# Attention's probabilities scaled by their reciprocal sums before the transposing instead of after the product with V

## Chip, cores and metric

One core of one Trainium2 chip. The metric is the device time of one execution in microseconds (us), as the median of three runs of the same program.

## What is computed

Two layers of a backbone over 1024 latent tokens with a prefix of 256 context tokens, all in float32. Each layer: modulated RMSNorm, one input projection split into retention, latent attention and pooling, an output projection, then a gated MLP with a convolution of width 3. Only the attention matters here. Eight heads; 1024 latent queries see 1280 keys (256 context, 1024 latent), 256 context queries see the 256 context keys. In layer 1 only the latent queries are needed.

```python
def mla_attend(qn, qr, kn, kr, v):
    s = jnp.einsum('bhqd,bhkd->bhqk', qn, kn) + jnp.einsum('bhqr,bkr->bhqk', qr, kr)
    p = jax.nn.softmax(s.astype(jnp.float32) * MLA_SCALE, axis=-1)
    return jnp.einsum('bhqk,bhkd->bhqd', p.astype(v.dtype), v)
```

## The kernel before

Every float32 product is made of reduced-precision parts: an operand is split into a high part (a copy rounded to fp32r) and a low part (the difference), and TensorE multiplies the parts.

**The unit.** `attention` (L1640) works in units of one head and 256 queries, which are two tiles t = 0, 1 of 128 queries. Layer 0 has 40 units (five per head: four latent, one context), layer 1 has 32 (four per head). For a latent unit:

- `S0`, `S1`, `SC` (`score`, L1689, which calls `mm3`, L187): the scores with queries on partitions, into PSUM: `SL[t]` for the 1024 latent keys of one tile, `SC` for the 256 context keys of both tiles. There is one buffer of each.
- `M0`, `M1`, `MC` (L1708, L1711): row maxima on VectorE. `B0`, `B1` (L1716): the bias of the exponential from them.
- `X0`, `X1` (`expo`, L1722): ScalarE's exponentials into `P`, 128 x 1280 in SBUF, with the row sums as a by-product.
- `T00`, `T01`, `T10`, `T11`, `T12` (`trans`, L1738): TensorE turns P round in blocks of 128 x 128 into a PSUM tile `pt`; the first digit is the query tile, the second the group of four key blocks; `T12` takes the context keys of both tiles. `H..` (L1761): ScalarE's high part of `pt`. `L..` (L1766): VectorE's low part.
- `AVa`, `AVb`, `AVc` (`av`, L1789): 20 products with V into the PSUM tile `O` (V's high and low part side by side give 128 output rows).
- `RC`, `DG`, `RR`: the sums are put together and inverted on VectorE (L1772, L1774); GpSimd splits the inverses and puts them on a diagonal (L1782 to L1784); two matmuls with ones (L1806) spread them over 64 partitions, beside `O`.
- `LO` (L1812): ScalarE copies the lower half of `O`. `OU` (`out`, L1814): VectorE adds the halves (L1817) and multiplies by the spread inverses (L1822) into `op`.
- `PAh`, `PAl` (L1833, L1841): for an odd head, the high and low part of `op` for the output projection. `PAl` runs on VectorE and reads two tiles in SBUF.

`pt` and `O` share three PSUM banks in turn; every third allocation falls on the same bank.

**The order** is written out by hand in `ORDERS`: a string of `name:k`, where k is the unit's distance from the first unit of the step. A step covers two units in layer 1 and five in layer 0. Each engine takes its part of that string strictly in the order written. So around one unit TensorE does `AVc` of the unit before, three groups of transposing with `SC` of the next unit between or ahead of them, `S1` of the next unit, two groups of transposing, `AVa`, `S0`, `AVb`. GpSimd does nothing else in this stage, and no DMA is issued by it there; SyncE's queue loads the next head's Q, K and V.

Of the kernel before, what the change touches and what calls it, by code (L numbers as in the profile page):

```python
# [8 lines left out]
F32 = mybir.dt.float32  # L9
F32R = mybir.dt.float32r  # L10
AF = mybir.ActivationFunctionType
ALU = mybir.AluOpType
# [5 lines left out]
SEQ = 1024  # L18
CTX = 256
T = SEQ + CTX  # L20
# [37 lines left out]

ORDERS = (
# [15 lines left out]
)  # L75


# [84 lines left out]
class Net:  # L162
# [325 lines left out]
    def run(self):  # L488
        tc = self.tc
        with ExitStack() as es:  # L490
            es.enter_context(tc.manual_schedule())
            P = lambda name, bufs=1, **k: es.enter_context(tc.tile_pool(name=name, bufs=bufs, reuse_waits="tile", **k))
            self.cpool = P("const")
            self.big = P("big")
            self.wpool = P("w", 2)
            self.dram = es.enter_context(tc.tile_pool(name="dram", bufs=1, space=DRAM))
# [1143 lines left out]
    def attention(self, l):  # L1640
        tc, nc, a = self.tc, self.nc, self.a
        lat = l == L - 1
        Tq = self.Tq
        Y = self.Y
        with ExitStack() as es:
            ga = es.enter_context(tc.tile_pool(name="ga", bufs=1, reuse_waits="tile"))
# [4 lines left out]
            SC = pS.tile([128, 2, 256], F32, name="SC")  # L1651

            units = []
# [23 lines left out]
            st = Units()  # L1677

            def begin(u):
                s = type("U", (), {})()  # L1680
                s.P = [None, None]
                s.sm = ga.tile([128, 12], F32, tag="sm", name="sm", bufs=3)
# [6 lines left out]
            def score(u, t, out, kc, n):  # L1689
                h, q0, _ = units[u]  # L1690
                q, k, _ = heads[h]
                qs = slice(q0 + t * 128, q0 + t * 128 + 128)
                self.mm3(out, q[0][:, qs], q[1][:, qs], k[0][:, kc:kc + n], k[1][:, kc:kc + n], True, True)
# [28 lines left out]
            def expo(u, t):  # L1722
                s = st[u]
                sm = s.sm
                P = s.P[t] = ga.tile([128, T], F32, tag="P", name="P", bufs=3)
                b = sm[:, 4 + t:5 + t]
                if units[u][2]:
                    nc.scalar.activation(P[:, 0:SEQ], SL[t], AF.Exp, scale=ATT_SCALE, bias=b,
                                         accum_out=sm[:, 6 + t:7 + t])
                nc.scalar.activation(P[:, SEQ:T], SC[:, t], AF.Exp, scale=ATT_SCALE, bias=b,  # L1730
                                     accum_out=sm[:, 8 + t:9 + t])
# [33 lines left out]
                    hi, lo, ps = st[u].t[t, g]  # L1765
                    nc.vector.tensor_tensor(out=lo, in0=ps, in1=hi.bitcast(F32), op=ALU.subtract)  # L1766

            def recip(u):
                sm = st[u].sm
                src = sm[:, 8:10]  # L1770
                if units[u][2]:
                    nc.vector.tensor_tensor(out=sm[:, 6:8], in0=sm[:, 6:8], in1=src, op=ALU.add)  # L1772
                    src = sm[:, 6:8]
                nc.vector.reciprocal(out=sm[:, 10:12], in_=src)  # L1774

            def diag(u):

                s = st[u]
                rr = ga.tile([128, 2, 2], F32R, tag="rr", name="rr", bufs=2)
                s.dg = ga.tile([128, 2, 2, 128], F32R, tag="dg", name="dg", bufs=2)  # L1780
                r = s.sm[:, 10:12]
                nc.gpsimd.tensor_copy(rr[:, 0], r)  # L1782
                nc.gpsimd.tensor_tensor(out=rr[:, 1], in0=r, in1=rr[:, 0].bitcast(F32), op=ALU.subtract)
                nc.gpsimd.tensor_tensor(out=s.dg.rearrange("p i t q -> p (i t) q"),  # L1784
                                        in0=self.ident[:, None, :].to_broadcast([128, 4, 128]),
                                        in1=rr.bitcast(F32).rearrange("p i t -> p (i t)")[:, :, None].to_broadcast([128, 4, 128]),
                                        op=ALU.mult)

            def av(u, g):  # L1789
                s = st[u]  # L1790
# [8 lines left out]
                    nc.tensor.matmul(s.O[:, 0:256], v[:, k], s.pl[:, k], start=False, stop=k == 9)  # L1799
                    s.open = k < 9  # L1800

            def rep(u):

                s = st[u]
                for i in range(2):
                    nc.tensor.matmul(s.O[0:64, 256:512], self.onesr, s.dg[:, i].rearrange("p t q -> p (t q)"),  # L1806
                                     start=not s.open and i == 0, stop=not s.open and i == 1)

            def low_out(u):
                s = st[u]  # L1810
                s.t1 = ga.tile([64, 256], F32, tag="t1", name="t1", bufs=2)
                nc.scalar.activation(s.t1, s.O[64:128, 0:256], AF.Copy)  # L1812

            def out(u):  # L1814
                s = st[u]
                h, q0, _ = units[u]
                nc.vector.tensor_tensor(out=s.t1, in0=s.O[0:64, 0:256], in1=s.t1, op=ALU.add)  # L1817
                if h % 2 == 0 and q0 == 0:
                    st["op"] = ga.tile([128, Tq], F32, tag="op", name="op")
                op = ops["op", u] = st["op"]  # L1820
                r = slice(64 * (h % 2), 64 * (h % 2) + 64)
                nc.vector.tensor_tensor(out=op[r, q0:q0 + 256], in0=s.t1, in1=s.O[0:64, 256:512], op=ALU.mult)  # L1822
                del st[u]

            def part_high(u):
# [9 lines left out]
            def part_low(u):  # L1835
                h, q0, _ = units[u]
                op = ops.pop(("op", u))
                if h % 2 == 1:
# [9 lines left out]
                   "M0": lambda u: max_lat(u, 0), "M1": lambda u: max_lat(u, 1), "MC": max_ctx,  # L1848
                   "B0": lambda u: bias(u, 0), "B1": lambda u: bias(u, 1),
                   "X0": lambda u: expo(u, 0), "X1": lambda u: expo(u, 1),  # L1850
                   "RC": recip, "DG": diag, "RR": rep, "LO": low_out, "OU": out,
                   "PAh": part_high, "PAl": part_low}
            for g in range(3):
                ops["AV" + "abc"[g]] = lambda u, g=g: av(u, g)
# [425 lines left out]
```

## Time and profile before

| what | value |
|---|---|
| median of three runs | 3344.43 us (3340.59 to 3345.43) |
| the profiled execution: time, span | 3334.97 us, 3333.2 us |
| TensorE, mean granted clock | 0.968 |
| busy: PE, PEld, DVE, ACT, POOL | 95%, 80%, 64%, 39%, 12% |
| chain that ended last: PE, DVE, ACT, POOL | 78%, 10%, 5%, 2% |
| attention of layer 0 | 498.5 to 794.4 us |
| attention of layer 1 | 2219.2 to 2489.5 us |

PE is TensorE (matmul), PEld its weight loads, DVE VectorE, ACT ScalarE, POOL GpSimd, SP SyncE. In the lists, `out<-in` names the tiles by the program's names and L1806 is a line of the kernel. The bounds of the two attention stages are where the first and last of their instructions stand in the list by time.

### The profile page before, as it was taken

To read this page: it belongs to the slowest core of one execution; us is meant where nothing else is said; L and a number is where in the kernel's file an instruction comes from. 1 tells how busy PE (TensorE), PEld (TensorE's weight loads), DVE (VectorE), ACT (ScalarE), POOL (GpSimd) and SP (SyncE) were. 2 spreads that over 40 slices of the span, in tenths; PEclk is the share of its full clock that TensorE was granted. 3 is DMA by queue.
4 is the path that set the end of the run, shared out by engine and by line. 5 is a ranking of instruction groups with operands and counts; after the bars stand their busy time and mean duration, and the time that the engine had idled before them with its cause. 6 is when DMAs were issued, how large, how long until landed. Compare 5 with 4: busy or idle time off the path is not lost.

```text
span 3333.2 us, 43486 instructions
## 1 busy us (share of the span) xinstructions
PE 3171.5 (95%) x16873; PEld 2676.0 (80%) x16873; DVE 2143.8 (64%) x3720; ACT 1291.3 (39%) x2277; POOL 413.1 (12%) x557
## 2 busy tenths in 40 slices
PE   7989789999999999999999899789999999999998
PEld 4767668998878888888888787579988788888887
DVE  6434768987667666666665745669985655555556
ACT  7443447774332222222222423457762422222222
POOL 3550221121310000000000300221112100000000
PEclk8999869999999999999999999879999999999999
DMA  6531643222212222222221322542223111111111
GB/s 227 178 120 52 243 114 82 64 67 99 76 46 62 64 64 64 64 64 64 64 64 39 105 88 85 205 117 77 68 85 89 58 48 48 48 48 48 48 48 73
DMA packets 307464, 280.27 MB, mean 84 GB/s; under 512 B 28880, under 2 KB 274874, under 8 KB 307258
## 3 DMA queue, kind: packets, MB, share of 16 engines
q1 hardware_dynamic: 292778, 228.65, 23.3%
q0 software_dynamic: 9152, 35.91, 2.7%
q10 hardware_dynamic: 5328, 12.93, 1.0%
q8 instruction: 133, 2.18, 0.3%
q14 instruction: 73, 0.60, 0.1%
HBM read 219.51 MB, written 57.93 MB: 83 GB/s over the span
## 4 chain that ended last, share of the span: by engine, by line
PE 78%; DVE 10%; ACT 5%; issue 3%; POOL 2%; DMA 2%; SPq 0%; DVEq 0%; POOLq 0%; ACTq 0%
PE up L203 30%; PE ip L826 8%; PE dn L189 5%; PE dn L190 5%; PE dn L191 5%; PE pt L1745 4%; PE O L1798 2%; PE O L1799 2%; PE SL L189 2%; PE SL L190 2%; PE SL L191 2%; PE wo L189 2%; PE wo L191 2%; PE wo L190 2%; DMA mraw<-in_w_mod_dram 1%
## 5 line engine op out<-in xcount | busy, mean ns | idle before, releaser
L2086 DVE SCALAR_TENSOR_TENSOR x<-dn,mod,x 128x512 f32<-128x512 f32 (+1 forms) x448 | 306.1, 687 | 401.8 <-PE dn L191 401.4
L189 PE MATMUL dn<-ah,dh 128*128 128x512 f32 (+1 forms) x800 | 295.2, 369 | 2.6 <-DVE x L2086 2.6
L190 PE MATMUL dn<-al,dh 128*128 128x512 f32 (+1 forms) x800 | 294.7, 368 | 0.0
L191 PE MATMUL dn<-ah,dl 128*128 128x512 f32 (+1 forms) x800 | 294.4, 368 | 0.0
L203 PE MATMUL up<-yml,whi 128*128 128x512 f32 (+1 forms) x840 | 254.6, 368 | 0.0
L203 PE MATMUL up<-ym,wlo 128*128 128x512 f32 (+1 forms) x840 | 254.4, 368 | 0.0
L203 PE MATMUL up<-ym,whi 128*128 128x512 f32 (+1 forms) x840 | 254.4, 368 | 0.0
L2037 ACT ACTIVATE t<-up,vecs 128x1280 f32<-128x1280 f32 (+2 forms) x92 | 116.0, 1265 | 307.6 <-PE up L203 297.6
L2046 DVE SCALAR_TENSOR_TENSOR t<-up,vecs,t 128x1023 f32<-128x1023 f32 (+2 forms) x135 | 134.4, 995 | 144.4 <-ACT t L2037 144.3
L203 PE MATMUL up<-yp,whi 128*128 128x512 f32 (+1 forms) x840 | 220.6, 369 | 0.0
L203 PE MATMUL up<-yr,whi 128*128 128x512 f32 (+1 forms) x840 | 215.0, 370 | 5.1 <-ACT whi L178 5.1
L1766 DVE TENSOR_TENSOR ptl<-pt,pth 128x512 fp32r<-128x512 f32 x328 | 214.3, 681 | 1.3 <-ACT pth L1761 0.2
L251 POOL TENSOR_TENSOR wlo<-raw,whi 128x512 fp32r<-128x512 f32 (+1 forms) x10 | 16.4, 1659 | 1579.7 <-ACT whi L250 1579.7
L1761 ACT ACTIVATE pth<-pt 128x512 fp32r<-128x512 f32 x328 | 184.7, 600 | 44.1 <-PE pt L1745 40.7
L179 DVE TENSOR_TENSOR wlo<-raw,whi 128x1024 fp32r<-128x1024 f32 (+1 forms) x134 | 163.6, 1221 | 56.4 <-ACT whi L178 56.4
L1745 PE MATMUL pt<-cpack,P 128*128 128x128 f32 x1312 | 180.9, 275 | 3.6 <-DVE op L1822 2.5
L402 DVE SCALAR_TENSOR_TENSOR macc<-mraw,sc,macc 128x128 f32<-128x128 f32 x560 | 175.1, 357 | 7.0
L203 PEld LDWEIGHTS up<-ym,wlo 128*128 128x128 f32 x840 | 158.4, 189 | 26.2
L203 PEld LDWEIGHTS up<-ym,whi 128*128 128x128 f32 x840 | 158.4, 189 | 26.2
L203 PEld LDWEIGHTS up<-yml,whi 128*128 128x128 f32 x840 | 158.3, 189 | 26.0
L189 PEld LDWEIGHTS dn<-ah,dh 128*128 128x128 f32 x800 | 150.7, 188 | 32.9 <-issue 5.6
L203 PEld LDWEIGHTS up<-yr,whi 128*128 128x128 f32 x840 | 150.9, 189 | 30.7 <-ACT whi L178 5.9
(405 smaller groups left out, 7661.8 us busy)
## 6 DMA issues: line engine op xcount, KB each, us to landing
raw<-in_w_up_dram SPq DMA_DIRECT2D x88, 512.0 KB
mraw<-in_w_mod_dram SPq DMA_DIRECT2D x56, 512.0 KB
draw<-in_w_down_dram SPq DMA_DIRECT2D x80, 256.0 KB
mraw<-in_w_mod_dram SPq DMA_DIRECT2D x96, 128.0 KB
raw<-in_w_in_dram SPq DMA_DIRECT2D x22, 512.0 KB
vsp<-ve POOLq DMA_DIRECT2D x20, 512.0 KB, 3.0
kh<-ksp SPq DMA_DIRECT2D x32, 320.0 KB
vh<-vsp SPq DMA_DIRECT2D x16, 640.0 KB
```

The source lines that it names most:

```text
L179: self.nc.vector.tensor_tensor(out=lo, in0=src, in1=hi.bitcast(F32), op=ALU.subtract)
L189: mm(ps, wh, rh, start=first, stop=False)
L190: mm(ps, wh, rl, start=False, stop=False)
L191: mm(ps, wl, rh, start=False, stop=last)
L203: mm(ps[:, c0:c0 + n], w(k), r(k)[:, c0:c0 + n], start=k == 0 and i == 0, stop=k == K - 1 and i == 2)
L402: nc.vector.scalar_tensor_tensor(out=acc[:, v], in0=raw[:, k], scalar=self.sc[:, k, v:v + 1], in1=acc[:, v], op0=ALU.mult, op1=ALU.add)
L826: mm(ps[:, c0:c0 + n], x, y[:, c0:c0 + n], start=j == 0, stop=j == 3 * K - 1)
L1745: nc.tensor.transpose(ps[:, i], s.P[tt][:, k * 128:k * 128 + 128], self.ident)
L1761: nc.scalar.activation(hi, ps, AF.Copy)
L1766: nc.vector.tensor_tensor(out=lo, in0=ps, in1=hi.bitcast(F32), op=ALU.subtract)
L2046: stt(out=t[:, f:e], in0=ps[:, f - 1:e - 1], scalar=V.cw0[:, m:m + 1], in1=t[:, f:e], op0=ALU.mult, op1=ALU.add)
L2086: stt(out=x, in0=ps, scalar=g2[:, m, v:v + 1], in1=x, op0=ALU.mult, op1=ALU.add)
```

## The change

Each tile of P (128 queries by 1280 keys) is multiplied in place by the inverses of its own row sums, by GpSimd, before it is turned round. The names `RC`, `DG` and `RR` go: no diagonal, no spreading matmuls. Two new names come, `N0` and `N1`, one for each query tile. Each adds the two partial sums on GpSimd (latent units alone), inverts 128 x 1 on VectorE, and multiplies P on GpSimd (`tensor_scalar`, 1280 columns for a latent unit, 256 for a context unit). `out` becomes one addition. P has four buffers instead of three.

The orders are rewritten. `N0` stands behind `M1`, `N1` behind `M0` of the unit after and ahead of `AVc`. The two latent groups of query tile 0 are now turned first; the third group is `T10`, in both layers. In layer 0 the fourth latent unit of a head has `S0` of a later unit between `N1` and `T10`; in the others `AVc`, `SC` and two groups of transposing stand there. The string of layer 0 is cut here; its last part and the places of `PAl` are told in the prediction where they matter.

```diff
 ORDERS = (
     (2,
-     "RC:0 T00:0 LO:-1 DG:0 PAh:-2 SC:1 OU:-1 H00:0 T10:0 MC:1 T11:0 H10:0 L00:0 S1:1 H11:0 B0:1 L10:0 X0:1 "
-     "T12:0 L11:0 T01:0 M1:1 AVa:0 H01:0 PAh:-1 S0:2 L01:0 H12:0 B1:1 PAl:-2 X1:1 L12:0 AVb:0 PAl:-1 M0:2 "
-     "RR:0 AVc:0 SC:2 RC:1 LO:0 DG:1 OU:0 T01:1 T00:1 H01:1 MC:2 T10:1 H00:1 S1:2 B0:2 L01:1 H10:1 X0:2 L00:1 "
-     "T11:1 L10:1 T12:1 M1:2 AVa:1 H11:1 H12:1 S0:3 B1:2 L11:1 X1:2 L12:1 AVb:1 M0:3 RR:1 AVc:1"),
+     "T00:0 LO:-1 PAh:-2 SC:1 OU:-1 H00:0 T01:0 MC:1 T10:0 H01:0 L00:0 S1:1 H10:0 B0:1 L01:0 X0:1 T12:0 "
+     "L10:0 T11:0 M1:1 N0:1 AVa:0 H11:0 PAh:-1 S0:2 L11:0 H12:0 B1:1 PAl:-2 X1:1 L12:0 AVb:0 PAl:-1 M0:2 "
+     "N1:1 AVc:0 SC:2 LO:0 OU:0 T01:1 T00:1 H01:1 MC:2 T10:1 H00:1 S1:2 B0:2 L01:1 H10:1 X0:2 L00:1 T11:1 "
+     "L10:1 T12:1 M1:2 N0:2 AVa:1 H11:1 H12:1 S0:3 B1:2 L11:1 X1:2 L12:1 AVb:1 M0:3 N1:2 AVc:1"),
     (5,
...
@@ expo
-                P = s.P[t] = ga.tile([128, T], F32, tag="P", name="P", bufs=3)
+                P = s.P[t] = ga.tile([128, T], F32, tag="P", name="P", bufs=4)
@@ recip, diag
-                    nc.vector.tensor_tensor(out=sm[:, 6:8], in0=sm[:, 6:8], in1=src, op=ALU.add)
-                nc.vector.reciprocal(out=sm[:, 10:12], in_=src)
-                nc.gpsimd.tensor_copy(rr[:, 0], r)
-                nc.gpsimd.tensor_tensor(out=rr[:, 1], in0=r, in1=rr[:, 0].bitcast(F32), op=ALU.subtract)
-                nc.gpsimd.tensor_tensor(out=s.dg.rearrange("p i t q -> p (i t) q"),
...
+            def norm(u, t):
+                s = st[u]
+                sm = s.sm
+                lat = units[u][2]
+                r = sm[:, 10 + t:11 + t]
+                if lat:
+                    nc.gpsimd.tensor_tensor(out=r, in0=sm[:, 6 + t:7 + t], in1=sm[:, 8 + t:9 + t], op=ALU.add)
+                nc.vector.reciprocal(out=r, in_=r if lat else sm[:, 8 + t:9 + t])
+                P = s.P[t] if lat else s.P[t][:, SEQ:T]
+                nc.gpsimd.tensor_scalar(out=P, in0=P, scalar1=r, scalar2=None, op0=ALU.mult)
@@ rep
-                    nc.tensor.matmul(s.O[0:64, 256:512], self.onesr, s.dg[:, i].rearrange("p t q -> p (t q)"),
-                                     start=not s.open and i == 0, stop=not s.open and i == 1)
@@ out
-                nc.vector.tensor_tensor(out=s.t1, in0=s.O[0:64, 0:256], in1=s.t1, op=ALU.add)
-                nc.vector.tensor_tensor(out=op[r, q0:q0 + 256], in0=s.t1, in1=s.O[0:64, 256:512], op=ALU.mult)
+                nc.vector.tensor_tensor(out=op[r, q0:q0 + 256], in0=s.O[0:64, 0:256], in1=s.t1, op=ALU.add)
```

## Rows read from the trace of the kernel before

**Rows 1.** Busy time of each engine in the two attention stages, layer 0 and layer 1.
```profile
core 0: us, PE busy (x) PEld busy (x) DVE busy (x) ACT busy (x) POOL busy (x), PEclk, DMA share, GB/s
498.50:794.40 295.90, 287.46 (x2037) 261.09 (x2038) 261.28 (x521) 229.71 (x517) 56.74 (x120) 0.99 0.29 77
2219.20:2489.50 270.30, 267.88 (x1903) 245.39 (x1903) 240.17 (x458) 206.45 (x463) 45.40 (x96) 0.99 0.27 73
```

**Rows 2.** PE's waits, 2240 to 2490 us: line waited for, us in total, times, longest.
```profile
PE pt L1745 <- DVE op L1822: 0.6, 1, 0.6
```

**Rows 3.** PE by time, layer 1: start, length, line, operation, operands; two units' spreading matmuls.
```profile
2357.72 0.40 PE L1806 MATMUL O<-dg,onesr 128*64 128x256 f32 x2
2357.95 0.28 PE L1798 MATMUL O<-pth,vh 128*128 128x256 f32 x1
...
2358.44 0.60 PE L1745 MATMUL pt<-cpack,P 128*128 128x128 f32 x4
2359.60 1.09 PE L1745 MATMUL pt<-cpack,P 128*128 128x128 f32 x8
2360.44 0.47 PE L189 MATMUL SL<-kh,qh 96*128 96x512 f32 x1
...
2366.07 0.40 PE L1806 MATMUL O<-dg,onesr 128*64 128x256 f32 x2
```

**Rows 4.** DVE's output product by line, attention of layer 0: xcount, busy us, mean ns.
```profile
L1822 DVE TENSOR_TENSOR op<-t,O 64x256 f32<-64x256 f32 x40 | 16.5, 413 | 1.4
```

**Rows 5.** POOL's groups by line and shape, whole span: xcount, busy us, mean ns.
```profile
L1784 POOL TENSOR_TENSOR dg<-cpack,rr 128x512 fp32r<-128x512 f32 x72 | 74.8, 1040 | 5.6
...
L1783 POOL TENSOR_TENSOR rr<-sm,rr 128x2 fp32r<-128x2 f32 x72 | 14.0, 195 | 5.8
L1782 POOL CAST rr<-sm 128x2 fp32r<-128x2 f32 x72 | 13.3, 184 | 467.1 <-DVE sm L1774 467.1
...
L1086 POOL MEMSET pw<- 128x128 f32 x4 | 0.8, 203 | 0.0
...
L1080 POOL MEMSET xp<- 128x8 f32 x4 | 0.4, 102 | 82.9 <-DVE kq L1155 64.8 <-PE pp L191 18.0
```

**Rows 6.** DVE, then POOL, then ACT, by time, in the unit of rows 3.
```profile
2357.04 1.23 DVE L1708 TENSOR_REDUCE sm<-SL 128x1 f32<-128x1024 f32 x1 [0.18 <-PE SL L191]
2358.18 0.15 DVE L1772 TENSOR_TENSOR sm<-sm 128x2 f32<-128x2 f32 x1
2358.37 0.17 DVE L1774 RECIPROCAL sm<-sm 128x2 f32<-128x2 f32 x1
...
2358.60 0.18 POOL L1782 CAST rr<-sm 128x2 fp32r<-128x2 f32 x1 [6.60 <-DVE sm L1774]
...
2357.16 0.20 ACT L1730 ACTIVATION_READ_ACCUMULATOR P<-SC,sm 128x1 f32 x1
```

**Rows 7.** DVE instructions beside a POOL instruction, by time, both layers.
```profile
788.76 1.04 POOL L1784 TENSOR_TENSOR dg<-cpack,rr 128x512 fp32r<-128x512 f32 x1
788.94 1.13 DVE L1841 TENSOR_TENSOR yml<-op,ym 128x256 fp32r<-128x256 f32 x1
...
2226.82 1.04 POOL L1784 TENSOR_TENSOR dg<-cpack,rr 128x512 fp32r<-128x512 f32 x1
2227.25 0.20 DVE L1716 TENSOR_SCALAR sm<-sm 128x1 f32<-128x1 f32 x1
```

**Rows 8.** DVE by time in a half step with two PAl, layer 1.
```profile
2363.63 0.69 DVE L1766 TENSOR_TENSOR ptl<-pt,pth 128x512 fp32r<-128x512 f32 x1
...
2364.36 0.42 DVE L1841 TENSOR_TENSOR yml<-op,ym 128x256 fp32r<-128x256 f32 x1
...
2365.63 1.22 DVE L1708 TENSOR_REDUCE sm<-SL 128x1 f32<-128x1024 f32 x1
```

**Rows 9.** The first unit of layer 1, by time: DVE's maximum, PE's second and third transposing.
```profile
2223.52 1.22 DVE L1708 TENSOR_REDUCE sm<-SL 128x1 f32<-128x1024 f32 x1 [2.57 <-PE SL L191]
...
2224.77 1.04 PE L1745 MATMUL pt<-cpack,P 128*128 128x128 f32 x8
```

More of the change, by code (lines that the diff above doesn't have):

```diff
@@ L1766, in low @@
                     nc.vector.tensor_tensor(out=lo, in0=ps, in1=hi.bitcast(F32), op=ALU.subtract)
[L1768 to L1771, printed above, removed]
-                    nc.vector.tensor_tensor(out=sm[:, 6:8], in0=sm[:, 6:8], in1=src, op=ALU.add)
-                    src = sm[:, 6:8]
-                nc.vector.reciprocal(out=sm[:, 10:12], in_=src)
-            def diag(u):
-                s = st[u]
-                rr = ga.tile([128, 2, 2], F32R, tag="rr", name="rr", bufs=2)
-                s.dg = ga.tile([128, 2, 2, 128], F32R, tag="dg", name="dg", bufs=2)
-                r = s.sm[:, 10:12]
-                nc.gpsimd.tensor_copy(rr[:, 0], r)
-                nc.gpsimd.tensor_tensor(out=rr[:, 1], in0=r, in1=rr[:, 0].bitcast(F32), op=ALU.subtract)
-                nc.gpsimd.tensor_tensor(out=s.dg.rearrange("p i t q -> p (i t) q"),
-                                        in0=self.ident[:, None, :].to_broadcast([128, 4, 128]),
-                                        in1=rr.bitcast(F32).rearrange("p i t -> p (i t)")[:, :, None].to_broadcast([128, 4, 128]),
-                                        op=ALU.mult)
+            def norm(u, t):
+                s = st[u]
+                sm = s.sm
[6 more added lines that the diff above has]
+                nc.gpsimd.tensor_scalar(out=P, in0=P, scalar1=r, scalar2=None, op0=ALU.mult)
             def av(u, g):
@@ L1800, in av @@
                     s.open = k < 9
-            def rep(u):
-                s = st[u]
-                for i in range(2):
-                    nc.tensor.matmul(s.O[0:64, 256:512], self.onesr, s.dg[:, i].rearrange("p t q -> p (t q)"),
-                                     start=not s.open and i == 0, stop=not s.open and i == 1)
             def low_out(u):
@@ L1850, in attention @@
                    "X0": lambda u: expo(u, 0), "X1": lambda u: expo(u, 1),
-                   "RC": recip, "DG": diag, "RR": rep, "LO": low_out, "OU": out,
+                   "N0": lambda u: norm(u, 0), "N1": lambda u: norm(u, 1), "LO": low_out, "OU": out,
                    "PAh": part_high, "PAl": part_low}
```

18 rows, old and new, of the table ORDERS are left out of this document.

## Prediction

> **What bounds it now.** I began with the busy times of the two attention stages [rows 1]. PE is busy 287 of 296 us in layer 0 and 268 of 270 us in layer 1, at a granted clock of 0.99 (the upper level, 2.4 GHz). DVE is next with 261 and 240 us, ACT follows, and POOL has 57 and 45 us. So these stages end when PE has done its list, and the reader should ask of each edit whether it shortens that list or makes PE wait. PE's waits say how little room is left: in layer 1 one real wait, 0.6 us, for the bank that the output step frees [rows 2]. The list of PE's work by time gives the unit: the spreading matmuls start at 2357.72 and again at 2366.07 [rows 3], 8.35 us a unit, with no gap between.
>
> **What PE loses.** The two spreading matmuls hold PE from 2357.72 to 2357.95, 0.23 us [rows 3]; their listed 0.40 us overlaps what follows. There are 72 pairs, one a unit. PE has nothing else to put there and nothing waits inside, so the whole comes off: 72 x 0.23 = **16.6 us**.
>
> **What DVE loses.** The product in the output step goes, 0.413 us a unit [rows 4], the sum moves to POOL, and one inversion of 0.17 us [rows 6] becomes two. DVE is not the bound, so I credit 0; a little of the 8 us that PE idles in layer 0 [rows 1] might come back. With less to do, DVE will more often wait for PE ahead of a maximum, as it does at 2357.04 [rows 6]. The output step also frees its bank one DVE operation earlier. The fourth buffer of P costs space alone. No DMA moves, and no queue of SP or POOL holds one in this stretch.
>
> **What POOL gets: the unknown price.** No row shows a POOL `tensor_scalar`. It reads one stream of 1280 elements and writes one. Below: writing alone, MEMSET, goes from 102 ns for 8 columns to 203 for 128 [rows 5], 0.84 ns an element, so 0.10 + 1272 x 0.84 = 1.17 us. Above: a two-stream operation whose operands repeat took 1040 ns for 512 and 195 for 2 [rows 5], 1.66 ns an element, so 2.31 us. I take the fixed part of the nearest one-stream operation (CAST, 184 ns) and the slope of MEMSET: **1.25 us**, since one read and one write need not share what two reads share. Two a unit plus two additions of 0.2 us make 2.9 us of 8.1 us, so POOL itself has room even at the upper price (5.0 us).
>
> **Is it in time?** Three deadlines.
> - *N0.* It stands behind M1, which ends at 2363.63 in rows 8; its tile is first wanted behind `AVc`, at 2366.07 + 0.49 = 2366.56 [rows 3]. Hidden at 1.25 us, and still at 2.31 us.
> - *N1.* This is the tight one. The inversion takes the place of L1772 at 2358.18, right behind the maximum that started when PE's scores were done. From an inversion's start to POOL's start took 0.23 us [rows 6]. So POOL multiplies from 2358.41 to 2359.66, and PE may read at about 2359.72 (0.06 us to hand over, as from the inversion's end to POOL). PE wants that tile at its third transposing: the pair of groups that starts at 2359.60 takes 0.84 us, to 2360.44 [rows 3], so the third group is at 2360.02, and 2359.79 without the spreading. That leaves **0.07 us**. At 1.25 us nothing is lost; each 0.1 us beyond 1.32 costs 0.1 us in each of the 56 units that have this pattern (32 in layer 1, three a head in layer 0), 5.6 us in all. The addition on POOL is not late: ACT's last sum is there at 2357.36 [rows 6], 0.8 us before the maximum ends. Behind a waiting inversion DVE would queue the output step and the maxima of the context scores, but it has no cause to wait.
> - *PAl.* The low part for the output projection reads two SBUF tiles on DVE. One of them began at 788.94 while POOL worked until 789.80, and took 1.13 us instead of 0.42 [rows 7, 8]: held until POOL was done, then 0.27 us more. In the new order the first `PAl` of a step meets N0's multiplication every time.
>
> The Trainium skill says of that last point (SBUF — State Buffer, section "Who interferes with whom") that a VectorE instruction with two SBUF inputs contends with a GpSimd instruction that reads SBUF, and that whoever comes first holds the ports for its whole length; the trace agrees, with 1.13 us for 0.42. It adds that a `tensor_scalar` can enter a two-port mode and be held as well: by that, the bias `B1` would wait 0.6 us for N0's multiplication in most units, an estimate of +34 us. The trace shows otherwise.
>
> The bias of the exponentials took its usual 0.20 us at 2227.25, in the middle of a POOL instruction [rows 7], so I charge nothing for it.
>
> What that lock costs: in the half step of rows 8 the maximum M1 ends at 2363.63. With the inversion ahead, POOL multiplies from 2363.86 to 2365.11; `L11` and `B1`, 0.73 us as before (2363.63 to 2364.36), are done by 2364.55; `PAl` waits and ends at 2365.38; `L12` (0.6 us) and the second `PAl` (0.33) put M0 at 2366.31 instead of 2365.63 [rows 8]. Its inversion comes 1.14 us later, and N1's product is ready at 2367.45 + 0.23 + 1.25 + 0.06 = 2368.99. `AVc` now starts at 2366.07, where the spreading stood [rows 3], and lasts 0.49 us; the third transposing is 1.58 us behind its end (2358.44 to 2360.02), at 2368.14. PE waits **0.85 us**. Layer 1 has 16 `PAl` (four odd heads of four units), two a half step, the last pair behind the scores: 7 x 0.85 = 6.0 us. In layer 0 three of them stand in one half step, 0.34 us more: 3 x 1.2 = 3.6 us. Together **9.6 us**. The bounds are 0 (they slip past POOL) and some 14 us (the `PAl` ahead of a `B1` in layer 0 counts too).
>
> **Filling.** In the first unit PE has no other work. The maximum of 2223.52 gives an inversion at 2224.66 [rows 9], a product at 2226.20; the third transposing stood at 2225.17. 1.0 us lost in layer 1, half taken for layer 0, whose first unit has more ahead of it: **1.5 us**.
>
> **Sum.** -16.6 + 9.6 + 1.5 = **-5.5 us** on the profiled execution's 3334.97 us. The median of the runs shown is 9.5 us above it; I carry the difference over to the median: 3344.4 - 5.5 = **3339 us**. About 0.2% (6.7 us) is what a measurement of this kernel can tell from no change, and this stands just inside.
>
> **The rivals.**
> - *All of it hides.* `PAl` slips past POOL, or POOL is nearer 1.17 us. For it: DVE gains 0.4 us a unit and may reach `PAl` at another time. Against: both follow from the same M1. -16.6 + 1.5 = -15 us: 3329 us.
> - *POOL becomes the bound through N1* (slower). If one stream with a scalar costs what the repeated operands cost, 2.31 us, N1 is ready at 2358.41 + 2.31 + 0.06 = 2360.78 against 2359.79: 1.0 us in 56 units. `PAl` is held 1.06 us longer in ten half steps and moves M0 by as much, so those ten cost 2.0 us more than the others. The filling becomes 3.6 us. -16.6 + 56 + 20 + 3.6 = +63 us: 3407 us. It decides from 1.32 us on, and takes the whole gain back by about 1.4 us. For it: every POOL arithmetic row of this size lies at 1.66 ns an element or above. Against: they all read two streams. The Trainium skill (GPSIMD Engine Reference, "Performance versus the Vector engine") speaks against the change: it calls GpSimd the wrong engine for ordinary elementwise work, at about 2.6 cycles an element; at its 1.2 GHz that is an estimate of 2.8 us here. Of a single input its section "When to use GPSIMD" says roughly line rate. No row before shows which holds.
> - *In between*: 1.4 to 1.8 us, for instance by an extra read of the scalar: 0.1 to 0.5 us in 56 units and twice that on top in the ten half steps: +2 to +33 us, 3347 to 3378 us.
>
> **Chances.** Forecast 0.50, with a range of its own of 3330 to 3348 us; all hides 0.20; in between 0.12; upper price 0.18. Faster by over 0.2%: nearly all of the second case and two fifths of the first, 0.39. Within 0.2%: 0.30. Slower: 0.31, from the last two cases. The range runs from all of the 16.6 us, 3327 us, to 3385 us; the upper price beyond it is the part left out.
>
> **What would show it.** No L1806; PE's third transposing (L1745, reading P of tile 1) waits for POOL's multiplication only in the half steps with `PAl`. A POOL `tensor_scalar` of 1.2 to 1.3 us. L1841 at about 0.8 us where it meets POOL. A unit of 8.12 us elsewhere. I am wrong if POOL's row is over 1.4 us, or if PE waits for POOL in most units, or if DVE's bias instructions lengthen beside POOL.

## The result, and the profile after

The changed kernel takes 3642.4 us (median of four runs, 3636.9 to 3647.7) against 3344.2 us for the kernel before on the same chip: a ratio of 1.0893, 95% interval 1.0875 to 1.0912. It is 298 us slower. The forecast of 3339 us and its whole range were wrong.

The two attention stages took nearly all of it. From the first to the last start of ScalarE's exponential over the context scores, layer 0 went from 285.4 to 457.1 us and layer 1 from 262.6 to 386.1 us: +171.7 and +123.5, together 295 of the 313 us that lie between the two profiled executions. Here are the busy times of the engines in those stages of the changed kernel, in the columns of [rows 1].

```profile
508.00:980.00 472.00, 350.07 (x1976) 306.29 (x1977) 258.91 (x494) 230.31 (x519) 253.12 (x144) 0.84 0.18 50
2402.00:2795.00 393.00, 303.79 (x1809) 268.90 (x1808) 243.33 (x424) 208.76 (x460) 235.91 (x128) 0.87 0.18 50
```

PE, once busy for nearly all of the stage, now idles 122 of 472 us and 89 of 393 us. POOL has gone from 57 and 45 us to 253 and 236, which is still little over half. And the granted clock has fallen from 0.99 to 0.84 and 0.87: part of the two stages ran at the lower level, 1.2 GHz. POOL's groups by line and shape give the price that [rows 5] had to bound.

```profile
L1778 POOL TENSOR_SCALAR P<-P,sm 128x1280 f32<-128x1280 f32 x128 | 453.1, 3540 | 129.0 <-DVE sm L1776 57.9 <-DVE sm L1716 32.2 <-DVE sm L1719 24.0
...
L1778 POOL TENSOR_SCALAR P<-P,sm 128x256 f32<-128x256 f32 x16 | 14.6, 924 | 51.0 <-DVE sm L1716 47.3 <-ACT pth L1761 3.6
```

The multiplication (now line 1778) takes 3.54 us, not 1.25, and lies over the upper bound of 2.31 us. From 256 to 1280 columns it is (3540 - 924) / 1024 = 2.55 ns an element. PE's waits, whole span, show who pays:

```profile
PE pt L1745 <- POOL P L1778: 193.6, 97, 4.3
```

Next come PE's transposings and scores by time in layer 1, the counterpart of [rows 3]. The two rows with a wait are `T10` of two successive units.

```profile
2599.95 1.12 PE L1745 MATMUL pt<-cpack,P 128*128 128x128 f32 x4 [3.02 <-POOL P L1778]
...
2613.15 1.12 PE L1745 MATMUL pt<-cpack,P 128*128 128x128 f32 x4 [2.11 <-POOL P L1778]
2613.92 0.78 PE L189 MATMUL SL<-kh,qh 96*128 96x512 f32 x1
2614.49 0.63 PE L190 MATMUL SL<-kh,qh 96*128 96x512 f32 x1
...
2616.63 0.63 PE L1745 MATMUL pt<-cpack,P 128*128 128x128 f32 x2
```

The unit is 13.2 us here, against 8.35 before. PE waits 2 to 3 us at the third group of transposing, and what follows the wait runs slowly: a score's six matmuls (`S1`) take from 2613.92 to 2616.63, 2.71 us, some 0.43 us each, against 0.23 before the change, as in these two rows of the kernel before:

```profile
2360.76 0.39 PE L190 MATMUL SL<-kh,qh 96*128 96x512 f32 x1
2360.99 0.40 PE L191 MATMUL SL<-kh,qh 96*128 96x512 f32 x1
```

This unit is one of those beside which the `PAl` of an odd head run, and the units are not alike. From 2489 us on a unit of layer 1 takes 11.2 to 11.9 us where no `PAl` runs, and 12.6 to 14.4 us where they do. Here is a stretch of four units of each kind, without and then with `PAl`, in the columns of [rows 1]:

```profile
2545.00:2589.00 44.00, 33.45 (x221) 29.60 (x220) 27.21 (x51) 24.17 (x54) 29.41 (x15) 0.96 0.21 55
2589.00:2645.00 56.00, 44.49 (x252) 39.77 (x251) 35.67 (x62) 28.68 (x65) 30.60 (x18) 0.82 0.20 50
```

PE idles 10.6 of 44 us in the first and 11.5 of 56 us in the second, but only in the second has the granted clock fallen far. What brings it down in the one and not in the other is not shown.

DVE by time shows the lock that the prediction foresaw, against 0.42 us in [rows 8], and right ahead of it a bias that was not held. POOL's rows of the same stretch follow.

```profile
2619.81 0.20 DVE L1716 TENSOR_SCALAR sm<-sm 128x1 f32<-128x1 f32 x1
2619.93 1.75 DVE L1824 TENSOR_TENSOR yml<-op,ym 128x256 fp32r<-128x256 f32 x1
```

```profile
2618.33 3.52 POOL L1778 TENSOR_SCALAR P<-P,sm 128x1280 f32<-128x1280 f32 x1 [1.61 <-DVE sm L1776]
2621.85 0.19 POOL L1775 TENSOR_TENSOR sm<-sm 128x1 f32<-128x1 f32 x1
2623.99 3.52 POOL L1778 TENSOR_SCALAR P<-P,sm 128x1280 f32<-128x1280 f32 x1 [1.95 <-DVE sm L1776]
```

### The profile page after: what moved, and what is told of

Its sections match the earlier page's. It is cut to its first block, busy times and chain, and to the rows that moved or that the text cites. A ratio compares the mean times of both kernels' runs of the same rounds, so it can differ in the third digit from the quotient of the medians.

```text
span 3646.0 us, 43279 instructions
## 1 busy us (share of the span) xinstructions
PE 3283.9 (90%) x16729; PEld 2759.2 (76%) x16729; DVE 2145.4 (59%) x3656; ACT 1294.1 (35%) x2277; POOL 800.8 (22%) x613
## 4 chain that ended last, share of the span: by engine, by line
PE 69%; POOL 11%; DVE 11%; ACT 4%; issue 2%; DMA 2%; SPq 0%; POOLq 0%; DVEq 0%; ACTq 0%
PE up L203 27%; POOL P L1778 10%; PE ip L826 7%; PE dn L189 5%; PE dn L190 5%; PE dn L191 5%; PE pt L1745 3%; PE wo L189 1%; PE SL L191 1%; PE SL L189 1%; PE SL L190 1%; PE wo L191 1%; PE wo L190 1%; DVE sm L1708 1%; PE Rps L159 1%
## 5 line engine op out<-in xcount | busy, mean ns | idle before, releaser
L1778 POOL TENSOR_SCALAR P<-P,sm 128x1280 f32<-128x1280 f32 (+1 forms) x144 | 467.7, 3249 | 180.0 <-DVE sm L1716 79.6
L1745 PE MATMUL pt<-cpack,P 128*128 128x128 f32 x1312 | 236.4, 326 | 197.1 <-POOL P L1778 193.6
L1745 PEld LDWEIGHTS pt<-cpack,P 128*128 128x128 f32 x1312 | 187.3, 169 | 236.8 <-POOL P L1778 224.1
L1708 DVE TENSOR_REDUCE sm<-SL 128x1 f32<-128x1024 f32 x128 | 156.6, 1223 | 76.3 <-PE SL L191 74.8
L1789 PE MATMUL O<-pth,vh 128*128 128x256 f32 x656 | 178.0, 305 | 0.7 <-ACT pth L1761 0.7
```

The source lines that it names most:

```text
L1708: nc.vector.reduce_max(out=st[u].sm[:, t:t + 1], in_=SL[t], axis=AX.X)
L1745: nc.tensor.transpose(ps[:, i], s.P[tt][:, k * 128:k * 128 + 128], self.ident)
L1778: nc.gpsimd.tensor_scalar(out=P, in0=P, scalar1=r, scalar2=None, op0=ALU.mult)
L1789: nc.tensor.matmul(s.O[:, 0:256], v[:, k], s.ph[:, k], start=k == f, stop=False)
```

## Experiments

The theories are these. A: POOL's price does it, through N1's deadline, with the clock as a consequence. Rivals: the new order or the extra hand-overs cost by themselves; N0 costs as much as N1; the fallen clock is the larger part; DVE, held by POOL at its instructions with two inputs, sets the time (C in the expectations). Unless another base is named, a diff is against the changed kernel.

### The order without the multiplication: e1_no_mult

```diff
-                nc.gpsimd.tensor_scalar(out=P, in0=P, scalar1=r, scalar2=None, op0=ALU.mult)
+                del P
```

> The changed kernel without GpSimd's multiplication; its addition and VectorE's inversion stay, so the output is not divided by the sums. Theory A (all of the loss hangs on the multiplication's 3.52 us: PE waits for it at the third transposing and its clock falls there): the time falls below that of before by the spreading matmuls, 3344 - 16.6, with 0.5 to 1.5 us for the filling: 3326 to 3331 us. Rival B (the new order, the hand-over between three engines or the small additions cost by themselves): it stays above 3350 us. Rival C (DVE, held at its two-input instructions by POOL): the same as A, since nothing holds it now, so A and C are told apart by the next run.

Measured: 3322.6 us, ratio to the kernel before 0.9937 (0.9922 to 0.9951). The new order, the sums on POOL and the split inversions cost nothing that shows; without the multiplication the change is worth some 20 us, rather more than the 16.6 us of the spreading. Everything from 3323 us upwards is the multiplication's. What the extra 3 to 5 us are was not tried.

### What the price belongs to: e7_probe

Single instructions on a scratch tile, one in every second unit of the kernel before; the diff is shown without the conditions and without the lines for DVE and ACT:

```diff
...
+                        nc.gpsimd.tensor_scalar(out=pa, in0=pa, scalar1=pr, scalar2=None, op0=ALU.mult)
...
+                        nc.gpsimd.tensor_scalar(out=pa[:, 240:480], in0=pa[:, 0:240], scalar1=pr, scalar2=None, op0=ALU.mult)
...
+                        nc.gpsimd.tensor_scalar(out=pa, in0=pa, scalar1=0.5, scalar2=None, op0=ALU.mult)
...
+                        nc.gpsimd.tensor_copy(pa[:, 240:480], pa[:, 0:240])
...
+                        nc.gpsimd.tensor_tensor(out=pa, in0=pa, in1=pr.to_broadcast([128, 480]), op=ALU.mult)
...
```

> The kernel before, with seven single instructions on a scratch tile of ones in attention of layer 1, one every two units, to read their durations: POOL tensor_scalar by a 128x1 scalar over 480 columns in place, and over 240 from one half to the other; by a constant over 480; POOL copy over 240; POOL tensor_tensor with the scalar repeated over 480; VectorE tensor_scalar and ScalarE Copy with the scalar as scale over 480. If 2.5 ns an element belongs to tensor_scalar as an operation: 1.5, 0.88 and 1.5 us for the three of its forms. If it belongs to the scalar being fetched: 1.5, 0.88 and 0.6 us. If to working in place: 1.5, 0.4 and 1.5 us. The copy 0.4 us by CAST and MEMSET; tensor_tensor 1.0 us; VectorE 0.3 to 0.6 us; ScalarE 0.5 us. The time of the kernel is not of use.

POOL's groups by line and shape; the mean is ns of one, and each ran once:

```profile
L1875 POOL TENSOR_SCALAR pa<-pa,pr 128x480 f32<-128x480 f32 x1 | 1.5, 1492 | 0.0
...
L1879 POOL TENSOR_SCALAR pa<-pa 128x480 f32<-128x480 f32 x1 | 1.4, 1412 | 0.0
L1883 POOL TENSOR_TENSOR pa<-pa,pr 128x480 f32<-128x480 f32 x1 | 1.0, 987 | 0.0
...
L1877 POOL TENSOR_SCALAR pa<-pa,pr 128x240 f32<-128x240 f32 x1 | 0.9, 886 | 0.0
...
L1870 POOL MEMSET pa<- 128x480 f32 x1 | 0.5, 497 | 0.0
L1881 POOL COPY pa<-pa 128x240 f32<-128x240 f32 x1 | 0.4, 383 | 0.0
```

The scalar's source (a column or a constant, 1492 against 1412 ns) makes little difference. Nor does working in place: from 240 columns out of place to 480 in place the slope is (1492 - 886) / 240 = 2.5 ns, that of the large one. The same product as a `tensor_tensor` with the scalar repeated takes 987 ns, two thirds of it, and a plain copy of 240 columns 383 ns. So the price is that of the operation `tensor_scalar` on POOL; the number of streams does not set it. DVE took 464 ns and ACT 694 ns for the same 480 columns.

### The price changed: e2_384 and e3_bcast

`e2_384` multiplies 384 of the 1280 columns of a latent tile, to bring the instruction to the forecast's 1.25 us. `e3_bcast` does the whole product with the cheaper operation.

```diff
+                if lat:
+                    P = P[:, 0:384]
                 nc.gpsimd.tensor_scalar(out=P, in0=P, scalar1=r, scalar2=None, op0=ALU.mult)
```

```diff
-                nc.gpsimd.tensor_scalar(out=P, in0=P, scalar1=r, scalar2=None, op0=ALU.mult)
+                n = T if lat else CTX
+                nc.gpsimd.tensor_tensor(out=P, in0=P, in1=r.to_broadcast([128, n]), op=ALU.mult)
```

> The changed kernel with the multiplication over 384 of a latent tile's 1280 columns (the rest of P is left undivided). From the two rows of the changed kernel, 924 ns for 256 and 3540 for 1280, this takes 1.25 us, the price that the prediction assumed. Theory A with the prediction's deadlines: 3339 us (3330 to 3348), PE waits for POOL only in the half steps with PAl, L1824 about 0.8 us there. If the deadline of 1.32 us was itself wrong, or the lock of PAl larger, it lies above 3350 us with waits in most units. Rival C: POOL busy 2.9 us a unit, DVE held less, 3335 to 3345 us, with PE waiting for DVE's parts and not for POOL.

> The changed kernel with the same multiplication written as tensor_tensor with the inverse repeated along the row. From 1040 ns for 512 columns and 195 for 2 before, 2.31 us instead of 3.52. Theory A with the clock kept up: 1.0 us in 56 units and the prediction's other terms, 3407 us. Theory A with the clock falling in each wait as in the changed kernel: up to 2.9 us a unit more, 3410 to 3570 us, nearer the lower end if the waits are too short to bring the clock down. Rival C: POOL 5.0 us a unit, and DVE held for 2.3 instead of 3.5 us; the time would fall by 10 to 20 us only.

Measured: `e2_384` 3347.3 us, ratio 1.0018 (1.0009 to 1.0027), inside the expected range and 8 us over its middle. Its POOL group, PE's waits (layer 0, then layer 1), and the group of `PAl` on DVE in layer 1:

```profile
L1780 POOL TENSOR_SCALAR P<-P,sm 128x384 f32<-128x384 f32 x128 | 162.0, 1266 | 89.0 <-DVE sm L1776 27.9 <-PE O L1792 25.6 <-DVE sm L1719 18.1
```

```profile
PE pt L1745 <- POOL P L1780: 22.5, 35, 2.0
...
PE pt L1745 <- POOL P L1780: 2.4, 2, 1.2
```

```profile
L1826 DVE TENSOR_TENSOR yml<-op,ym 128x256 fp32r<-128x256 f32 x14 | 5.8, 416 | 0.0
```

At 1.27 us the deadlines of layer 1 hold as worked out: two waits, the filling among them. `PAl` is not held at all (416 ns mean); it slips past POOL. But layer 0 has 35 waits, four or five a head, where one head passes to the next. Three of the four at one such turn, and POOL's queue between them, by time:

```profile
612.58 1.53 PE L1745 MATMUL pt<-cpack,P 128*128 128x128 f32 x12 [0.45 <-POOL P L1780]
...
619.09 0.55 PE L1745 MATMUL pt<-cpack,P 128*128 128x128 f32 x3 [0.40 <-POOL P L1780]
...
623.83 0.66 PE L1745 MATMUL pt<-cpack,P 128*128 128x128 f32 x4 [0.54 <-POOL P L1780]
```

```profile
617.20 1.83 POOL L1780 TENSOR_SCALAR P<-P,sm 128x256 f32<-128x256 f32 x2 [4.68 <-DVE sm L1716]
619.03 0.19 POOL L1775 TENSOR_TENSOR sm<-sm 128x1 f32<-128x1 f32 x1
619.59 1.25 POOL L1780 TENSOR_SCALAR P<-P,sm 128x384 f32<-128x384 f32 x1 [0.37 <-DVE sm L1716]
```

The waits have more than one cause. The first of the turn, 0.80 us at 608.45, is `T00` of the head's fourth latent unit: the order of layer 0 has it ahead of `AVc` (`AVa:2 M1:3 N0:3` and later `T00:3 AVc:2`), so `N0`'s deadline is earlier there than the one that the prediction worked out. At 612.58 PE waits for the `N1` of that unit, at 619.09 for the context unit's own second product, at 623.83 for the `N1` of the next head's first unit. The context unit's two products, 1.83 us, also stand ahead of the next latent unit's addition, but that costs it under 0.1 us: ScalarE's last sum for it is there at 618.95, and it starts at 619.03. The prediction had given the turn of a head no cost: it counted three units a head by the pattern of layer 1 and left out the other two.

`e3_bcast`: 3442.6 us, ratio 1.0295 (1.0277 to 1.0312), 36 us above what the rival "POOL becomes the bound through N1" gave, 3407 us at 2.31 us, with a granted clock of 0.94 in layer 0. How the 36 us divide was not tried. Its rows, the POOL group and PE's waits over the whole span:

```profile
L1779 POOL TENSOR_TENSOR P<-P,sm 128x1280 f32<-128x1280 f32 x128 | 299.8, 2342 | 101.3 <-DVE sm L1776 55.3 <-DVE sm L1719 22.2 <-PE O L1791 21.4
```

```profile
PE pt L1745 <- POOL P L1779: 94.4, 78, 3.0
```

So the time follows the price: 3323 us at nothing, 3347 at 1.27, 3443 at 2.34, 3642 at 3.54. Rival C falls with these two runs: PE waits for POOL in both, and `e3_bcast` is 200 us faster than the changed kernel where C gave 10 to 20 us.

### One half at a time: e5_only_n0 and e6_only_n1

```diff
-                nc.gpsimd.tensor_scalar(out=P, in0=P, scalar1=r, scalar2=None, op0=ALU.mult)
+                if t == 0 or not lat:
+                    nc.gpsimd.tensor_scalar(out=P, in0=P, scalar1=r, scalar2=None, op0=ALU.mult)
```

`e6_only_n1` has `t == 1` there. Both keep the context unit's two products. A2 in the expectations is theory A with a ring through POOL's queue, which `e4_fill` (next section) had shown by then.

> The changed kernel with the multiplication for query tile 0 alone in latent units (tile 1 is left undivided, its addition and inversion stay). Theory A2 (the chain is a ring through POOL's queue: third transposing, ScalarE's high part, X0, N0's multiplication, then N1's addition and multiplication queued behind it, then the next third transposing; 4.1 us and two multiplications, 11.2 us as in the run with the filled wait): without N1 the ring is broken, PE is late for the first transposing alone, by the row of the half step (2363.86 + 3.52 against 2366.56) some 0.9 us, in a ring of 8.6 us instead of 8.1: 3340 to 3370 us. Rival (N1's deadline behind M0 is all): as without any multiplication, 3320 to 3328 us.

> The changed kernel with the multiplication for query tile 1 alone in latent units (tile 0 is left undivided). Theory A2: nothing stands ahead of N1 on POOL, the ring through M0 is 6.8 + 3.5 = 10.3 us at the full clock, 2.2 us over PE's own 8.1, and the clock falls in such waits: 3322 + 64 x 2.2 = 3463 us at least, and with 1 to 2 us of slow products 3500 to 3590 us, below the changed kernel's 3642 in any case. Rival (N1's deadline behind M0 is all): as the changed kernel, 3630 to 3650 us.

Measured: N0 alone 3434.4 us (1.0271, 1.0254 to 1.0289), N1 alone 3597.5 us (1.0759, 1.0735 to 1.0784). Both are above what theory A2 gave, N0 alone by 64 us. N1 alone brings 275 of the 320 us between `e1_no_mult` and the changed kernel, so it is the main one; but N0 is not hidden, with 112 us by itself. PE's wait in layer 0 of `e5_only_n0`:

```profile
PE pt L1745 <- POOL P L1779: 55.4, 37, 3.3
```

By the prediction's own deadline N0 had to be late: it starts at 2363.86 and at 3.54 us its product is readable at 2367.46, 0.9 us after 2366.56. I had tried that deadline at 1.25 and 2.31 us, not above. In layer 1 it fits: 16 waits, nearly all of 0.6 to 0.9 us. But layer 0, by the span of its context exponentials as above, has 82 of the 112 us, and 41 of its 55 us of waits are 15 waits of 2.2 to 3.3 us at the turns of the heads, such as these:

```profile
627.75 0.66 PE L1745 MATMUL pt<-cpack,P 128*128 128x128 f32 x4 [3.09 <-POOL P L1779]
...
641.87 0.66 PE L1745 MATMUL pt<-cpack,P 128*128 128x128 f32 x4 [2.19 <-POOL P L1779]
```

They are `T00` of the fourth latent unit, ahead of `AVc` as said above, and `T00` of the next head's first unit, behind the short context unit. This run also has `PAl` held for 2.81 us at 2508.11 in layer 1, and a granted clock of 0.91 in layer 0; their shares were not taken apart.

### The clock: e4_fill and e10_n1_fill

PE gets work while it waits: 20 transposings of the identity into the tile that `T10` then overwrites, in the changed kernel and in `e6_only_n1`.

```diff
+                if (t, g) == (1, 0):
+                    for _ in range(20):
+                        nc.tensor.transpose(ps[:, 0], self.ident, self.ident)
```

> The changed kernel with 20 more transposings of the identity ahead of each third group of transposing (T10), into the bank that this group then overwrites: 2.2 us of PE work at the full clock where PE now waits. Theory A, with the fallen clock as a cost of its own (a unit is 13.2 us; the chain from T10 round to the next T10 is 6.8 + 3.5 = 10.3 us at the full clock, so 2.9 us are the slower scores and products behind the wait): granted clock in the stage above 0.95, units of 10.3 to 10.6 us, time 3470 to 3510 us although work is added. If the fallen clock costs nothing (all of the 13.2 us is the chain with POOL): no faster than 3642 us, or slower by up to 140 us.

> The kernel of e6_only_n1 (the changed kernel without the multiplication of query tile 0 in latent units, so its values are not the reference's), with 20 transposings of the identity ahead of each T10, into a PSUM tile that T10 then overwrites: PE has work while it waits for POOL. They take 2.05 us by the spacing of the transposings (0.103 us). Theory: in e6 the ring behind M0 (a wait of 2.2 us in 56 units, 124 us over the 3323 us without any multiplication) is one part, and the fallen clock (0.80 to 0.85 in its attention) the rest; with PE busy the clock stays at 0.96 and the time is 3435 to 3480 us, a unit of 10.3 us. Rival: what e6 has beyond the ring of 2.2 us are further waits that PE's clock has no part in; then the filling changes nothing, 3580 to 3615 us.

Measured: `e4_fill` 3588.3 us (1.0731), `e10_n1_fill` 3490.7 us (1.0443, 1.0428 to 1.0458). The busy times of 200 us of layer 1, first of `e6_only_n1`, then of `e10_n1_fill`, columns as in [rows 1]:

```profile
2360.00:2560.00 200.00, 162.20 (x924) 143.02 (x923) 121.54 (x220) 106.48 (x234) 62.08 (x49) 0.83 0.25 65
```

```profile
2360.00:2560.00 200.00, 198.89 (x1496) 184.23 (x1495) 140.79 (x262) 125.04 (x282) 74.09 (x57) 1.00 0.23 59
```

With PE kept busy the granted clock is 1.00 instead of 0.83, and the kernel with *more* instructions is 107 us faster. The unit is then 10.4 us (the filling starts at 2604.41 and again at 2614.81; a unit is 10.3 or 10.6 us in most of layer 1), near the 10.3 us of N1's deadline. The time is 11 us over the expected range; 20 us of PE's waits for POOL are left in it, and the filling lasts 2.35 us instead of 2.05.

The same filling in the changed kernel took back 54 us alone, and my expectation of 3470 to 3510 us was a miss. At the full clock another ring holds: POOL's queue. POOL by time in `e4_fill`:

```profile
2605.99 3.52 POOL L1781 TENSOR_SCALAR P<-P,sm 128x1280 f32<-128x1280 f32 x1 [0.45 <-DVE sm L1716]
2609.49 0.19 POOL L1778 TENSOR_TENSOR sm<-sm 128x1 f32<-128x1 f32 x1
2610.04 3.52 POOL L1781 TENSOR_SCALAR P<-P,sm 128x1280 f32<-128x1280 f32 x1 [0.37 <-DVE sm L1779]
2616.54 0.19 POOL L1778 TENSOR_TENSOR sm<-sm 128x1 f32<-128x1 f32 x1 [2.98 <-ACT P L1730]
2617.18 3.52 POOL L1781 TENSOR_SCALAR P<-P,sm 128x1280 f32<-128x1280 f32 x1 [0.45 <-DVE sm L1779]
```

From one N0 to the next it is 11.2 us: two products of 3.52 with an addition and an inversion between (to 2613.56), and 3.6 us back. `T10` may start at 2613.62; ScalarE's `H10` waits for it and takes 0.60 us from 2614.31; the exponentials `X0` stand behind `H10` in ScalarE's order, and their last sum is what the next N0 addition waits for. N0's product delays N1's addition, and with it the inversion, on POOL's queue. The changed kernel itself goes round in this time where no `PAl` runs; two of its N0 products in turn are 11.2 us apart:

```profile
2545.22 3.52 POOL L1778 TENSOR_SCALAR P<-P,sm 128x1280 f32<-128x1280 f32 x1 [0.45 <-DVE sm L1776]
...
2556.40 3.52 POOL L1778 TENSOR_SCALAR P<-P,sm 128x1280 f32<-128x1280 f32 x1 [0.44 <-DVE sm L1716]
```

In `e4_fill` every second unit with `PAl` takes 12.8 us instead of 11.2, at a granted clock of 1.00 in layer 1: there `PAl`, held by POOL on DVE, puts off the maximum ahead of `N1`.

So the 298 us come apart like this, each a difference of two medians: 3344 to 3323, the spreading and what went with it (-22); to 3491, N1's late product with the clock kept (+168); to 3588, N0 through POOL's queue (+98); to 3642, the fallen clock (+54). The split depends on the order: without N0 the clock took 107 us, and N0 then added 45. The shares of N1 and N0 hold what `PAl` and the turns of the heads add: of N1's 168 us, 89 lie in layer 0 and 74 in layer 1 by the spans of the context exponentials. The filling costs something itself, so the clock's shares are more likely too small than too large.

### A cheaper form: e8_layer1, e9_late_n0, e11_high_first, e12_before_high_first

`e8_layer1` is built on the kernel before: layer 0 as it was, layer 1 with the cheaper product (2.33 us), `T10` moved behind `S1`, `PAl` on POOL, and every unit in the same order. Its order of layer 1:

```diff
...
+    (1,
+     "T00:0 LO:-1 SC:1 OU:-1 H00:0 L00:0 PAh:-1 T01:0 MC:1 B0:1 H01:0 X0:1 L01:0 PAl:-1 S1:1 T10:0 M1:1 B1:1 "
+     "N0:1 T11:0 H10:0 T12:0 L10:0 S0:2 H11:0 L11:0 AVa:0 H12:0 L12:0 X1:1 AVb:0 M0:2 N1:1 AVc:0"),
...
```

`e9_late_n0` moves `N0:1` behind `L10:0`. `e11_high_first` instead puts the four products of AVa with P's high part ahead of the four with its low part, and `e12_before_high_first` does that to the kernel before, as a control.

> Layer 0 as before. In layer 1 the change with two differences: the multiplication as tensor_tensor with the inverse repeated (2.34 us), and a new order in steps of one unit in which the third group of transposing stands behind the next unit's S1, the products behind S0, and POOL does PAl. By the ring of theory A2 N1 is then ready about 0.3 us and N0 about 0.7 us ahead of PE, so PE has 8.12 us a unit and no wait: 32 x 0.23 = 7.4 us less than before, some 1 to 3 us of it lost in filling a longer pipeline: 3336 to 3342 us. If the order leaves a wait of x us a unit: 32 x more; at 1 us and a falling clock 3370 to 3400 us.

> The kernel of e8_layer1 (layer 1 alone normalises ahead of the transposing, with the two-stream multiplication of 2.33 us), with one edit: in layer 1's order the whole of N0 (addition, inversion, multiplication) stands behind the low part L10 instead of ahead of T11. Theory: in e8 the inversion of N0 (0.16 us with its gap 0.22) stands between the bias B1 and L10 on DVE, and PE waits 0.14 us a unit for L10; taking it out of there gives a unit of 8.10 us instead of 8.22: 32 x 0.13 = 4 us, so 3334 to 3338 us, 6 to 10 us under the kernel before. N0's product is then ready 0.1 us ahead of T00 and N1's about as much ahead of T10. Rival: POOL's queue is too late by then (N0 late moves N1 late behind it), PE waits 0.1 to 0.4 us at T00 or T10 in each unit, and the time is 3340 to 3352 us.

> The kernel of e8_layer1, with one edit in `av`: in AVa the four products with P's high part come first and the four with its low part behind them, instead of in turn. Theory: in e8 PE waits 0.14 us a unit in AVa for the low part L10 (behind the inversion of N0 on DVE), because the second matmul of AVa reads it; with the high part first the low part is wanted 0.35 us later (three matmuls of 0.117 us), the wait goes, no instruction of POOL moves, and the unit is 8.09 us instead of 8.22: 3334 to 3338 us, 6 to 10 us under the kernel before. Rival: the 0.13 us turns into a wait elsewhere, because N0, N1 and T00, T10 come closer together (in e9 the products of POOL were late at T00 when the unit was to be shorter): the unit stays at 8.2 us, 3338 to 3342 us.

> The kernel before with the same edit of `av` alone (in AVa the four products with P's high part first). Control for e11: PE has no wait in AVa in the kernel before (one real wait of 0.6 us in the attention of layer 1), so there is nothing to gain: 3341 to 3347 us. Rival: it pays by itself, 3334 to 3340 us, and what e11 gains is not the normalising's.

Measured, as ratios to the kernel before: `e8_layer1` 0.9992 (0.9983 to 1.0001; 3340.2 us), `e9_late_n0` 1.0012 (1.0002 to 1.0021), `e11_high_first` 0.9997 (0.9988 to 1.0007), the control 0.9996 (0.9987 to 1.0006). None beats the kernel before by what can be measured. With a product that is in time, in this order and in layer 1 alone, the change is worth next to nothing: the unit of `e8_layer1` is 8.22 or 8.29 us, about 0.1 under 8.35, since some 0.13 us a unit are lost again to a wait of PE's weight loads, of which PE feels a part (PEld waits in layer 1: of `e8_layer1`, then of `e11_high_first`):

```profile
PEld O L1805 <- DVE ptl L1764: 13.3, 30, 1.6
```

```profile
PEld O L1805 <- DVE ptl L1764: 13.3, 30, 1.6
```

I took it for a wait for the data of `L10` in AVa's second matmul. `e11_high_first` refutes that: AVa reads the low part three matmuls later, and the wait is the same to the tenth. It is L1805, AVa's *first* product, which reads only the high part; what it can want of DVE there is the bank. `O` is the third allocation after `T10`, so it gets `T10`'s bank, which is free when `L10` has read it. That reading rests on this row and the allocation order; a kernel with another bank was not tried. `e9_late_n0` moved the inversion out of that path, but the weight loads still wait 11.7 us in 29 times, since `L10` then waits for ScalarE's `H10`:

```profile
2352.16 0.69 DVE L1764 TENSOR_TENSOR ptl<-pt,pth 128x512 fp32r<-128x512 f32 x1 [0.30 <-ACT pth L1759]
```

And it made N0's product late, as its rival said. POOL by time there, and PE's `T00`:

```profile
2353.06 2.32 POOL L1794 TENSOR_TENSOR P<-P,sm 128x1280 f32<-128x1280 f32 x1 [1.16 <-PE SL L189]
2355.34 0.19 POOL L1791 TENSOR_TENSOR sm<-sm 128x1 f32<-128x1 f32 x1
```

```profile
2355.44 0.66 PE L1743 MATMUL pt<-cpack,P 128*128 128x128 f32 x4
```

`T00` starts right behind the product's end at 2355.38, and the unit is 8.41 us.

## Why the prediction was wrong

- **The step that failed: POOL's price.** The prediction put an instruction that reads one stream between MEMSET's slope and that of an operation with repeated operands, and took 1.25 us, near the lower end. Measured 3.54 us. The upper bound was the price of *another* operation, and a good one for it: 2.31 us worked out, 2.34 measured in `e3_bcast`. For `tensor_scalar` it was no bound. I had listed as the argument against the rival that POOL's dearer rows all read two streams; `e7_probe` shows that streams don't order the prices. The estimate of 2.8 us, worked out from a figure of the Trainium skill (GPSIMD Engine Reference, "Performance versus the Vector engine"), was nearer than my number and still low. The Trainium skill's "roughly line-rate" for a single input (GPSIMD Engine Reference, "When to use GPSIMD") does not hold for this operation here: 2.55 ns an element.
- **N1's deadline: right in kind.** 1.32 us was the point from which it decides: at 1.27 us the steady units of layer 1 do not wait, and at 3.54 us the same line gives 2358.41 + 3.54 + 0.06 - 2359.79 = 2.2 us a unit, a unit of 10.3, where `e10_n1_fill` has 10.4. Over 56 units that is 124 us; with PE kept busy N1 cost 168. Most of the difference is layer 0's: 24 units of 2.2 us would be 53 us, and it has 89.
- **N0 "hidden": right only at the prices tried.** At 3.54 us it is 0.9 us late by the same deadline, and `e5_only_n0` is 112 us over `e1_no_mult`. At the turn of a head the deadline itself was wrong: `T00` of the fourth latent unit stands ahead of `AVc` and waits 0.80 us already at 1.27 us.
- **Missing: POOL's queue.** "POOL itself has room" weighed 5.0 us of work against 8.1. But N1's addition stands behind N0's product, and X0, which N0 waits for, behind `H10`, which waits for N1: a ring of 11.2 us with POOL idle a third of it.
- **Missing: the clock.** Each microsecond of PE's wait was costed as one. With waits of 2 to 3 us in a unit the granted clock fell to 0.84 and 0.87 over the two stages, not evenly (0.96 without `PAl` and 0.82 with it in the stretches shown). Where it fell, the work behind the wait ran at about half the rate: 54 to 107 us.
- **`PAl`: right in kind, mis-placed.** At 1.27 us it cost 0 instead of 9.6 us, the lower bound. In the changed kernel a `PAl` takes 0.40 to 2.58 us, with a mean of 0.94 us over 36; in `e4_fill` a half step with `PAl` in layer 1 is 1.6 us longer.
- **`B1`: right.** It took 0.20 us at 2619.81 in the middle of a POOL product (2618.33 to 2621.85). The rule of the Trainium skill (SBUF — State Buffer, "Who interferes with whom") by which it could have been held, which is tied there to conditions on the operands, did not show.
- **The spreading: right in sign, a little small.** 16.6 us forecast, some 20 without the multiplication.
- **Layer 0's turn of a head: missed.** 22.5 us at 1.27 us, in four or five waits a head: for `N0` at an early `T00`, for the `N1` of the units on either side, for the context unit's own product. With the price right, the sum would have been -22 + 25 = +3 us instead of -5.5, and `e2_384` shows it.

## What to carry to other kernels

The price of an operation on GpSimd is that operation's own: counting its streams bounds nothing, and a dearer operation can be replaced by a cheaper one with the same result (`tensor_tensor` with the scalar repeated, 2.34 us, for `tensor_scalar`, 3.54 us). If work moves to a slower engine inside the loop, draw the whole ring through that engine's queue, and try each deadline at twice the highest price, not only at the likely one. If the full engine would wait some microseconds in every round, add what its clock may lose, for the work after the wait pays too.

## What the runs showed of the hardware that was not expected

- GpSimd multiplies 128x1280 float32 by a scalar in 3.54 us, 2.55 ns an element, and by the same scalar as a repeated operand in 2.34 us; a copy of 240 columns takes 0.38 us, and a `tensor_scalar` of 240 columns 0.89.
- A kernel with 20 useless transposings in each latent unit is 107 us faster than the one that waits instead, at a granted clock of 1.00 against 0.83 in the stretch shown.
- PE's weight loads for the first product into `O` waited 13.3 us in 30 times for DVE's reading of another tile, and moving the reads of the data did not change that by a tenth of a microsecond. That the wait is for the PSUM bank is a reading, not shown.
- In the changed kernel PE idles 10.6 of 44 us at a granted clock of 0.96, and 11.5 of 56 us at 0.82.
